# Six output weights split by GpSimd and an adding transfer, and spare splits bound in order behind block splits, in a two-layer encoder kernel

## The chip, the cores and the metric

The kernel runs on one core of one Trainium2 chip. The metric is the device time of one execution in microseconds (us). Several executions of a kernel are timed; one further execution was recorded by the hardware profiler, and all views of the profile come from that one. The engines are named as in the profile: PE is TensorE (matmul), PEld its weight loads, DVE is VectorE, ACT is ScalarE, POOL is GpSimd, SP is SyncE, which here only issues transfers (DMAs).

## What is computed

Two layers of an encoder on 512 tokens of width 1024, all in fp32. Layer 0 mixes tokens by banded attention (mixer A), layer 1 by global attention (mixer B); both add attention over 256 memory rows, an output product with `w_o`, and a SwiGLU feed-forward part.

```python
for i in range(DEPTH):                                   # DEPTH = 2
    h = rms_norm(x, g_mix_pre[i])
    proj = h @ w_in[i]                                   # q, k, v, memory q
    tok = mixer_a(...) if i == 0 else mixer_b(...)       # 12 heads of 64, 3 kv heads
    mo = memory_attention(qm, km, vm)                    # 4 heads
    o = jnp.concatenate([tok, mo], axis=-1) @ w_o[i]
    x = x + rms_norm(o, g_mix_post[i])
    h = rms_norm(x, g_ffn_pre[i])
    gu = h @ w_gate_up[i]
    f = (jax.nn.silu(gu[..., :D_FF]) * gu[..., D_FF:]) @ w_down[i]   # D_FF = 2816
    x = x + rms_norm(f, g_ffn_post[i])
```

## The kernel before

**Splits.** Every fp32 operand of a large product is split into a high part, which is the operand rounded to the matmul's narrower format (`fp32r`), and a low part, which is what is left. A product is then three matmuls: high by high, high by low, low by high (`mm3`, L308 to L310; L1131 to L1133 and L1257 to L1259 in the feed-forward part). The helper `split` (L313) makes the parts: ACT copies the source into the high tile (L318), and DVE subtracts the high tile from the source (L322). A flag moves the first to POOL (L316) or the second (L320). The weights' parts are tiles `whi` and `wlo` with four buffers each, taken in turn, so a new pair waits until PE has done with the pair four before. The unsplit weight comes from HBM by a transfer that SP issues, into a tile `raw`.

**Order.** PE's instructions run in the order in which the program writes them. All other engines take their instructions in an order that a scheduler made ahead of time, and each engine works through its list strictly in order: an instruction that waits holds up all behind it. An edge `issue_after(a)` tells the scheduler to place an instruction behind `a`.

**Mixers.** In each layer the heads' pieces (scores, softmax, transposes, values) are laid on one axis `x`, one unit for a head, by `put(x, f)` and written out in that order. `PACE` holds the places for each layer. The first half of the output product (`heads_out`, L837) is laid among the last heads: four weight units `wo[0..3]` of 128 x 1024 are loaded and split by `unit` at `ow` = 10.3, 10.8, 12.2, 13.2 (layer 0), the second half of each split a quarter unit later, and `owm` picks the engines (0: ACT and DVE). The products with units 0 to 2 start at `ox` = 11.4; unit 3 is used in `mix_out`, after the heads. In layer 1, units 0 and 1 come ready split from HBM (below); only units 2 and 3 are split there. POOL's work in this stage is the softmax's division (L663, tile `p`), four instructions a head.

**Feed-forward.** The 22 columns of 128 hidden values are worked through in four lots (`LOTS`). Lots 1 and 2 use a seven-product scheme (`seven`, L1125, for the first product). Such a lot ends with `down(h)` (L1314), the second product by the same scheme: seven stages of `times` (L1252) named A11, A12, S2, S1, S3, S4, A22, each of 18 matmuls on `fp32r` parts of a weight block. The blocks `b11`, `b21`, `t2`, `t1`, `t3`, `b22`, `t4` come from HBM into tiles `rb`, `ru`, `raw` (1024 wide) and `rs` (512 wide), some as sums made by an adding transfer that POOL issues (L1082); `pairs` (L1243) splits each. The hidden values of the lot's last column are still made by ACT (SiLU, L1184; high part, L1007) and DVE while A12 begins; the last third of A12 needs them.

**Spare pairs, in layer 0 only.** While layer 0 runs, weights of layer 1 are loaded, split and stored as pairs in HBM, for layer 1 to fetch. In each of lots 1 and 2, `spare_load` (L1295) loads two units of `in_wq` into `raw` during A12, and `spare_pair` (L1302), twice, splits one unit in two halves through tiles `c` (high) and `s` (low), two buffers each, and stores the four halves (`pair<-c`, `pair<-s`). The split is the same helper, so its rows have lines L318 and L322 with tile names `c` and `s`. In `down` the two calls of `spare_pair` stand behind the products S1 and S4 (L1333 and L1340). After the lot's A22 the next lot begins with `p1` and `p2` (L1139, L1144), which need the pair `a`, split from `raw`.

Of the kernel before, what the change touches and what calls it, by code (L numbers as in the profile page):

```python
# [28 lines left out]
NF = DFF // P  # L29
EPS = 1e-6  # L30
NPART = 2
WPART = 2
BIG = 1e37
NFILL = 3
# [9 lines left out]
LOTS = ((0, 2), (2, 8), (8, 14), (14, 22))  # L44
SEVEN, HALF = (1, 2), 3

PACE = [{'lag': 1.692, 'vlag': 0.479, 'jstep': 0.213, 'kstep': 0.375, 'klag': 0.742, 'qoff': [0.212, 0.126, 0.099], 'qlag': 1.02, 'late': 0.6, 'moff': -0.235, 'mdur': 0.562, 'mlag': 0.697, 'kw': [0, 0, 0, 0], 'mw': [2, 1, 1, 0], 'qw': [0, 0, 0, 1, 3, 3, 3, 3], 'hoff': 0, 'ow': [10.3, 10.8, 12.2, 13.2], 'ox': 11.4, 'od': 0.3, 'hstep': 0.872, 'hlag': 1.742, 'hjstep': 0.135, 'hvlag': 0.751, 'owm': [0, 0, 0, 0, 0, 0, 0, 0], 'q0step': 0.27, 'q0off': -0.032, 'q0lag': 0.919, 'm0off': -0.078, 'm0dur': 0.002, 'm0lead': 1.887, 'mlead': 1.201, 'qlead': 0.921, 'q0lead': 1.555, 'qstep': 1.002, 'tw': [0, 0, 0, 0, 0, 0, 0, 0], 'h2off': 0}, {'lag': 1.824, 'vlag': 0.535, 'jstep': 0.218, 'kstep': 0.777, 'klag': 1.715, 'qoff': [-0.027, -0.162, -0.027], 'qlag': 1.189, 'late': 2.15, 'moff': -0.088, 'mdur': 0.384, 'mlag': 1.205, 'kw': [0, 0, 0, 0], 'mw': [0, 0, 0, 0], 'qw': [0, 0, 0, 0, 0, 3, 1, 1], 'hoff': 0, 'ow': [10.2, 10.7, 12.2, 13.2], 'ox': 11.3, 'od': 0.3, 'hstep': 0.946, 'hlag': 1.847, 'hjstep': 0.295, 'hvlag': 0.568, 'owm': [0, 0, 0, 0, 0, 0, 0, 0], 'q0step': 0.718, 'q0off': -0.018, 'q0lag': 1.136, 'm0off': -1.059, 'm0dur': 0.171, 'm0lead': 2.465, 'mlead': 3.162, 'qlead': 1.895, 'q0lead': 1.42, 'qstep': 0.998, 'tw': [0, 0, 0, 0, 0, 0, 0, 0], 'h2off': 0.016}]

# [155 lines left out]
class Trunk:  # L204
# [39 lines left out]
    def unit(self, src, side=0, pool=None, parts=1, put=None, x=0, dst=None, key=None, g=None, raw=None, pair=None, early=None):  # L244


        nc, n = self.nc, src.shape[-1]
        own = raw or self.early.pop(early, None)
        if pair in self.pairs:
            def fetch():  # L250
                dst[key] = [self.whl.tile([P, 1024], F32R, tag=z, name=f"w{z}", bufs=4) for z in ("hi", "lo")]
                for z in range(2):
                    nc.sync.dma_start(dst[key][z].bitcast(F32), self.pairs[pair][z])

            put(x, fetch)
# [612 lines left out]
    def mix_out(self, l, forms, resid, dst):  # L868
# [115 lines left out]
    def ffn(self, l, pools, forms, late, done):  # L984
# [235 lines left out]
        for k in range(2):  # L1220
            c = slice(512 * k, 512 * k + 512)
# [21 lines left out]
        def pairs(t):  # L1243
            out = []
            for x in t:
                n = x.shape[-1]
                hi, lo = [self.whl.tile([P, 1024], F32R, tag=z, name=f"w{z}", bufs=4) for z in ("hi", "lo")]
                self.split(hi[:, :n], lo[:, :n], x)
                out.append((hi, lo))
            return out  # L1250

        def times(ps, h, name, pr, steps, fresh):  # L1252
            mm = nc.tensor.matmul
            for i, t in steps:
                lh, ll = block(h["lot"], name, 0, i, t), block(h["lot"], name, 1, i, t)
                rh, rl = [pr[i // 2][z][:, i % 2 * 512:i % 2 * 512 + 512] for z in range(2)]
                mm(ps[t], lh, rh, start=fresh and i == 0, stop=False, skip_group_check=True)  # L1257
                mm(ps[t], lh, rl, start=False, stop=False, skip_group_check=True)  # L1258
                mm(ps[t], ll, rh, start=False, stop=i == HALF - 1, skip_group_check=True)  # L1259
# [42 lines left out]
        def spare_pair():  # L1302
            if spares:
                x, name, *at = spares.pop(0)
                self.pairs[(name, *at)] = y = [self.dram.tile([P, 1024], F32, name="pair", tag="_".join(map(str, (name, z, *at))))
                                               for z in range(2)]
                for z in range(2):
                    c = slice(512 * z, 512 * z + 512)
                    hi, lo = temp("c"), temp("s")
                    self.split(hi.bitcast(F32R), lo.bitcast(F32R), x[:, c])  # L1310
                    queue(nc.sync, y[0][:, c], hi)
                    queue(nc.sync, y[1][:, c], lo)

        def down(h):  # L1314

            x = h["x"]
            due()
            out_of(x, 0, 0)
            w = pairs(h["b21"])
            z = [self.tagged("s"), self.tagged("s")]  # L1320
            times(z, h, "A12", w, BY_UNIT, True)
            spare_load()
            spare_load()
            down_load(h, 3)
            rope()
            out_of(z, 0, 0)
            w = pairs(h["t2"])
            times(x, h, "S2", w, BY_UNIT, False)
            out_of(x, 0, 1, True)
            w = pairs(h["t1"])  # L1330
            y = [self.tagged("pv"), self.tagged("t")]
            times(y, h, "S1", w, BY_ROW, True)
            spare_pair()  # L1333
            out_of(y, 1, 1)
            w = pairs(h["t3"])
            times(x, h, "S3", w, BY_ROW, False)
            out_of(x, 1, 1, True)
            w = pairs(h["b22"])
            times(y, h, "S4", w, BY_ROW, False)
            spare_pair()  # L1340
            out_of(y, 0, 1)
            w = pairs(h["t4"])
            times(x, h, "A22", w, BY_ROW, False)
            out_of(x, 1, 0)

        for c, (f0, f1) in list(enumerate(LOTS))[1:]:
# [40 lines left out]
            if c in SEVEN:  # L1387
                down(head)
# [221 lines left out]
```

## Time and profile before

| | |
|---|---|
| median of 3 runs | 1089.26 us (1089.0 to 1090.06) |
| the profiled execution, as timed | 1091.68 us |
| its span in the profile | 1089.9 us |
| granted TensorE clock, mean over the span | 0.994 |
| busy: ACT, POOL | 693.5 us, 255.3 us |

A profile row of the timeline gives start, duration, engine, line, operation, output and inputs; in brackets stand the engine's idle time just before and what ended it. The table by windows gives each engine's busy time in a stretch, the number of instructions in brackets, then the clock granted to PE (1.00 is full), the busy share of the 16 DMA engines and GB/s. PE is busy nearly throughout, so a change of time is a change of PE's waits or of its clock.

### The profile page before, as it was taken

What the parts mean: (1) busy time and instruction counts of PE and PEld (TensorE: products, weight loads), DVE (VectorE), ACT (ScalarE), POOL (GpSimd) and SP (SyncE); (2) the same over time, 40 slices, a digit from 0 to 9 for tenths busy, and PEclk for the clock granted to TensorE, in tenths of its full rate; (3) what the DMA queues carried; (4) which work ended last, traced back from release to release, by engine and by line L of the source; (5) the groups of instructions that cost most, each with busy time, mean ns of one, the idle gap of its engine ahead of it and who ended that gap; (6) DMA issues with size and microseconds to landing.
All of it is one profiled execution on the core that took longest, in us unless ns stands there. A gap on an engine that the chain in (4) does not pass through costs nothing.

```text
span 1089.9 us, 19990 instructions
## 1 busy us (share of the span) xinstructions
PE 1063.6 (98%) x7364; PEld 973.2 (89%) x7364; DVE 894.2 (82%) x1561; ACT 693.5 (64%) x1429; POOL 255.3 (23%) x405
## 2 busy tenths in 40 slices
PE   9999999999999989999999999999999999999997
PEld 7899887999879979998898888778999899899986
DVE  7889875978899979995887998767979888899954
ACT  7679884766646645663566888766766466556631
POOL 5673331211131100000443553313011111100001
PEclk9999999999999999999999999999999999999999
DMA  9721106456987894329752220136369769833243
GB/s 326 265 67 39 33 20 258 148 134 173 264 272 181 233 273 166 110 67 317 242 193 98 78 78 1 47 119 227 104 149 261 219 162 255 220 113 105 68 162 116
DMA packets 56978, 173.42 MB, mean 159 GB/s; under 512 B 6576, under 2 KB 6960, under 8 KB 56752
## 3 DMA queue, kind: packets, MB, share of 16 engines
q1 hardware_dynamic: 47376, 150.76, 40.4%
q0 software_dynamic: 9216, 20.98, 11.4%
q8 instruction: 58, 0.95, 0.4%
q10 hardware_dynamic: 288, 0.40, 0.1%
q14 instruction: 40, 0.33, 0.1%
HBM read 149.04 MB, written 16.78 MB: 152 GB/s over the span
## 4 chain that ended last, share of the span: by engine, by line
PE 82%; DVE 7%; ACT 4%; DMA 3%; issue 2%; POOL 2%; SPq 0%; DVEq 0%; POOLq 0%; ACTq 0%
PE ps L1131 11%; PE ps L1132 11%; PE ps L1133 11%; PE ps L309 9%; PE ps L308 9%; PE ps L310 9%; PE ps L1259 3%; PE ps L1257 3%; PE ps L1258 3%; PE tp L673 3%; PE o L687 2%; PE o L688 2%; PE s L612 1%; DMA raw<-in_wq_dram 1%; PE s L613 1%
## 5 line engine op out<-in xcount | busy, mean ns | idle before, releaser
L318 ACT ACTIVATE whi<-raw 128x512 fp32r<-128x512 f32 (+3 forms) x180 | 141.2, 804 | 93.6 <-issue 26.0
L322 DVE TENSOR_TENSOR wlo<-raw,whi 128x512 fp32r<-128x512 f32 (+3 forms) x176 | 157.8, 912 | 38.3 <-ACT whi L318 37.8
L1131 PE MATMUL ps<-hrows,whi 128*128 128x256 f32 x640 | 176.3, 275 | 0.1
L1132 PE MATMUL ps<-hrows,wlo 128*128 128x256 f32 x640 | 176.2, 275 | 0.0
L1133 PE MATMUL ps<-hrows,whi 128*128 128x256 f32 x640 | 176.2, 275 | 0.0
L308 PE MATMUL ps<-whi,hrows 128*128 128x256 f32 (+2 forms) x432 | 144.1, 333 | 0.0
L309 PE MATMUL ps<-wlo,hrows 128*128 128x256 f32 (+2 forms) x432 | 138.0, 319 | 1.6 <-DVE wlo L322 1.5
L310 PE MATMUL ps<-whi,hrows 128*128 128x256 f32 (+2 forms) x432 | 138.0, 320 | 0.0
L1132 PE MATMUL ps<-a,wlo 128*128 128x256 f32 x480 | 132.1, 275 | 0.0
L1131 PE MATMUL ps<-a,whi 128*128 128x256 f32 x480 | 132.1, 275 | 0.0
L1133 PE MATMUL ps<-a,whi 128*128 128x256 f32 x480 | 132.1, 275 | 0.0
L1131 PEld LDWEIGHTS ps<-hrows,whi 128*128 128x128 f32 x640 | 120.1, 188 | 0.8 <-ACT p L1137 0.3
L1132 PEld LDWEIGHTS ps<-hrows,wlo 128*128 128x128 f32 x640 | 120.1, 188 | 0.5
L1133 PEld LDWEIGHTS ps<-hrows,whi 128*128 128x128 f32 x640 | 120.1, 188 | 0.0
L663 POOL TENSOR_SCALAR p<-p,rd 128x256 f32<-128x256 f32 (+2 forms) x128 | 78.1, 628 | 102.8 <-DVE rd L660 66.2
L1132 PEld LDWEIGHTS ps<-a,wlo 128*128 128x128 f32 x480 | 90.1, 188 | 0.2
L1131 PEld LDWEIGHTS ps<-a,whi 128*128 128x128 f32 x480 | 90.1, 188 | 0.2
L1133 PEld LDWEIGHTS ps<-a,whi 128*128 128x128 f32 x480 | 90.1, 188 | 0.0
L309 PEld LDWEIGHTS ps<-wlo,hrows 128*128 128x128 f32 x432 | 81.6, 189 | 7.4 <-DVE wlo L322 2.5
L310 PEld LDWEIGHTS ps<-whi,hrows 128*128 128x128 f32 x432 | 81.3, 188 | 5.6 <-DVE hrows L336 0.3
L308 PEld LDWEIGHTS ps<-whi,hrows 128*128 128x128 f32 x432 | 81.4, 188 | 5.0
L318 ACT ACTIVATE whi<-rb 128x1024 fp32r<-128x1024 f32 x56 | 59.6, 1064 | 29.9 <-PE ps L1259 20.7
(231 smaller groups left out, 2854.0 us busy)
## 6 DMA issues: line engine op xcount, KB each, us to landing
raw<-in_wgu_dram SPq DMA_DIRECT2D x48, 512.0 KB, 4.6
rb<-in_wgu_dram SPq DMA_DIRECT2D x40, 512.0 KB, 3.9
raw<-in_wd_dram SPq DMA_DIRECT2D x18, 512.0 KB, 4.3
raw<-in_wq_dram SPq DMA_DIRECT2D x16, 512.0 KB, 5.3
raw<-in_wo_dram SPq DMA_DIRECT2D x16, 512.0 KB, 3.6
rb<-in_ws_dram SPq DMA_DIRECT2D x16, 512.0 KB, 7.6
rs<-in_ws_dram SPq DMA_DIRECT2D x28, 256.0 KB, 6.5
xt<-x SPq DMA_DIRECT2D x12, 512.0 KB, 4.9
```

The costliest lines, as they stand in the source:

```text
L308: mm(out, lh, rh, start=first, stop=False)
L309: mm(out, lh, rl, start=False, stop=False)
L310: mm(out, ll, rh, start=False, stop=last)
L318: a = nc.scalar.activation(hi, src, AF.Copy)
L322: b = nc.vector.tensor_sub(lo, src, hi.bitcast(F32))
L663: self.pooled = nc.gpsimd.tensor_scalar(hd["p"][z][:, :n], hd["p"][z][:, :n], rd[:, z:z + 1], 1.0, op0=OP.mult, op1=OP.mult)
L673: nc.tensor.transpose(tp[:, z], hd["p"][i][:, jj * P:(jj + 1) * P], self.ident)
L1131: mm(out, wh[:, s], rh, start=start and k == 0, stop=False, skip_group_check=True)
L1132: mm(out, wl[:, s], rh, start=False, stop=False, skip_group_check=True)
L1133: mm(out, wh[:, s], rl, start=False, stop=k == 3, skip_group_check=True)
L1257: mm(ps[t], lh, rh, start=fresh and i == 0, stop=False, skip_group_check=True)
L1258: mm(ps[t], lh, rl, start=False, stop=False, skip_group_check=True)
```

## The change

**Output weights.** Units with `owm` = 4 take another way through `unit`: all four in layer 0, units 2 and 3 in layer 1, so six. At `x - 0.8` (`EARLY`) the tiles are taken and SP issues the load. Then, for each half, ACT copies the high part as before, and POOL writes the negative of the high part into the low tile. After the second half POOL issues an adding transfer that adds the raw weight (512 KB, from on-chip memory to on-chip memory) to the low tile. DVE has no part in it.

**Spare pairs.** In `down` the two calls of `spare_pair` move one place: behind `pairs(h["t3"])` and behind `pairs(h["t4"])`, so behind the lot's next block split instead of ahead of it. `pairs` and `spare_pair` keep the last split's two instructions in `ends["pair"]`, and each spare split is bound behind both by order edges.

```diff
+EARLY = 0.8
 PACE, layer 0:
-'owm': [0, 0, 0, 0, 0, 0, 0, 0]
+'owm': [4, 4, 4, 4, 0, 0, 0, 0]
 PACE, layer 1:
-'owm': [0, 0, 0, 0, 0, 0, 0, 0]
+'owm': [0, 0, 4, 4, 0, 0, 0, 0]
...
+        def turned_over():
+            hi, lo = dst[key] = [self.whl.tile([P, 1024], F32R, tag=z, name=f"w{z}", bufs=4) for z in ("hi", "lo")]
+            own = self.raw()
+            nc.sync.dma_start(own[:, :n], src)
+            box.append((hi, lo, own))
+
+        def high(z):
+            hi, lo, own = box[0]
+            c = slice(z * n // NPART, (z + 1) * n // NPART)
+            nc.scalar.activation(hi[:, c], own[:, c], AF.Copy)
+            nc.gpsimd.tensor_scalar(lo[:, c], hi[:, c].bitcast(F32), -1.0, 1.0, op0=OP.mult, op1=OP.mult)
+            if z == NPART - 1:
+                nc.gpsimd.dma_start(lo[:, :n], own[:, :n].bitcast(F32R), accum_op=OP.add, max_dma_last_dim=4096)
+
+        if side == 4:
+            put(x - EARLY, turned_over)
+            for z in range(NPART):
+                put(x - EARLY + 0.01 + z / 4, lambda z=z: high(z))
+            return
...
-                self.split(hi[:, :n], lo[:, :n], x)
+                ends["pair"] = self.split(hi[:, :n], lo[:, :n], x)
...
-                    self.split(hi.bitcast(F32R), lo.bitcast(F32R), x[:, c])
+                    a, b = ends["pair"]
+                    with self.tc.issue_after(a), self.tc.issue_after(b):
+                        ends["pair"] = self.split(hi.bitcast(F32R), lo.bitcast(F32R), x[:, c])
...
             times(y, h, "S1", w, BY_ROW, True)
-            spare_pair()
             out_of(y, 1, 1)
             w = pairs(h["t3"])
+            spare_pair()
             times(x, h, "S3", w, BY_ROW, False)
...
             times(y, h, "S4", w, BY_ROW, False)
-            spare_pair()
             out_of(y, 0, 1)
             w = pairs(h["t4"])
+            spare_pair()
             times(x, h, "A22", w, BY_ROW, False)
```

PE's list is the same row for row; what moves stands on the other engines. Lines behind the new code are 21 higher in the changed kernel up to `pairs` (so L322 becomes L343), and the new code is L297 (ACT), L298 and L300 (POOL).

ACT, in layer 0 at the end of lot 1, from the splits of `b21` on, before. `c<-raw` is a spare split, `whi<-ru` the split of `t2` and then of `t1`, `s<-ps` the SiLU of the lot's last column and `f<-s` the high part of its hidden values:

```order
L318 ACTIVATE whi<-rs 128x512
L318 ACTIVATE c<-raw 128x512
L318 ACTIVATE whi<-ru 128x1024
L1184 ACTIVATE s<-ps 128x256
L318 ACTIVATE whi<-rs 128x512
L1007 ACTIVATE f_4231<-s 128x512
L318 ACTIVATE c<-raw 128x512
L318 ACTIVATE whi<-ru 128x1024
```

The same place in the changed kernel, to the first two spare splits (the rows between are the splits of `t1` and `t3`):

```order
L339 ACTIVATE whi<-rs 128x512
L339 ACTIVATE whi<-ru 128x1024
L1205 ACTIVATE s<-ps 128x256
L339 ACTIVATE whi<-rs 128x512
L1028 ACTIVATE f_4235<-s 128x512
L339 ACTIVATE whi<-ru 128x1024
L339 ACTIVATE f_4242<-q 128x512
L1028 ACTIVATE f_4247<-k 128x256
L339 ACTIVATE whi<-rs 128x512
L339 ACTIVATE whi<-rb 128x1024
L339 ACTIVATE whi<-rs 128x512
L339 ACTIVATE c<-raw 128x512 x2
```

The two spare splits of the first call have moved from ahead of the SiLU and of `t1` to behind the split of `t3`. The second call's two stand in the changed kernel behind the splits of `t4`, just ahead of the next lot's `whi<-raw`. Lot 2 reads alike.

DVE, in layer 0's mixer among the last heads, where the output product begins, before. `tl<-tp,th` is the low part of a turned softmax tile, `p,nm` the masked scores, `tok` a head's result:

```order
L322 TENSOR_TENSOR hrows<-tok,hrows 128x512
L322 TENSOR_TENSOR wlo<-raw,whi 128x512
L322 TENSOR_TENSOR tl<-tp,th 128x256
L618 ISA p,nm<-s,mask,nsink 128x256
L618 ISA nm 128x1
L696 TENSOR_TENSOR tok<-o,tmp 64x512
L618 ISA p,nm<-s,mask,nsink 128x256
L618 ISA nm 128x1
L659 TENSOR_TENSOR den<-den,es 128x4
L322 TENSOR_TENSOR wlo<-raw,whi 128x512
L660 RECIPROCAL rd<-den 128x4
L322 TENSOR_TENSOR tl<-tp,th 128x384 x2
```

The same place in the changed kernel:

```order
L639 ISA p,nm<-s,mask,nsink 128x256
L639 ISA nm 128x1
L343 TENSOR_TENSOR tl<-tp,th 128x256
L717 TENSOR_TENSOR tok<-o,tmp 64x512
L639 ISA p,nm<-s,mask,nsink 128x256
L639 ISA nm 128x1
L680 TENSOR_TENSOR den<-den,es 128x4
L681 RECIPROCAL rd<-den 128x4
L343 TENSOR_TENSOR tl<-tp,th 128x384
```

The two weight splits are gone from DVE, and the split of a finished head (`hrows<-tok`) has moved further back, on ACT too.

POOL, in layer 0's mixer around the third and fourth output weight of the changed kernel (before, the rows L663 followed one another without any between):

```order
L684 TENSOR_SCALAR p<-p,rd 128x256
L298 TENSOR_SCALAR wlo<-whi 128x512 x2
L300 DMA wlo<-raw 128x1024
L684 TENSOR_SCALAR p<-p,rd 128x256
L684 TENSOR_SCALAR p<-p,rd 128x384 x2
L684 TENSOR_SCALAR p<-p,rd 128x256
L298 TENSOR_SCALAR wlo<-whi 128x512 x2
L684 TENSOR_SCALAR p<-p,rd 128x256
L684 TENSOR_SCALAR p<-p,rd 128x384 x2
L684 TENSOR_SCALAR p<-p,rd 128x256
L300 DMA wlo<-raw 128x1024
```

The new instructions stand between one head's four divisions and the next head's, and the fourth weight's transfer a head later than its negatives.

More of the change, by code (lines that the diff above doesn't have):

```diff
@@ L45 @@
 SEVEN, HALF = (1, 2), 3
-PACE = [{'lag': 1.692, 'vlag': 0.479, 'jstep': 0.213, 'kstep': 0.375, 'klag': 0.742, 'qoff': [0.212, 0.126, 0.099], 'qlag': 1.02, 'late': 0.6, 'moff': -0.235, 'mdur': 0.562, 'mlag': 0.697, 'kw': [0, 0, 0, 0], 'mw': [2, 1, 1, 0], 'qw': [0, 0, 0, 1, 3, 3, 3, 3], 'hoff': 0, 'ow': [10.3, 10.8, 12.2, 13.2], 'ox': 11.4, 'od': 0.3, 'hstep': 0.872, 'hlag': 1.742, 'hjstep': 0.135, 'hvlag': 0.751, 'owm': [0, 0, 0, 0, 0, 0, 0, 0], 'q0step': 0.27, 'q0off': -0.032, 'q0lag': 0.919, 'm0off': -0.078, 'm0dur': 0.002, 'm0lead': 1.887, 'mlead': 1.201, 'qlead': 0.921, 'q0lead': 1.555, 'qstep': 1.002, 'tw': [0, 0, 0, 0, 0, 0, 0, 0], 'h2off': 0}, {'lag': 1.824, 'vlag': 0.535, 'jstep': 0.218, 'kstep': 0.777, 'klag': 1.715, 'qoff': [-0.027, -0.162, -0.027], 'qlag': 1.189, 'late': 2.15, 'moff': -0.088, 'mdur': 0.384, 'mlag': 1.205, 'kw': [0, 0, 0, 0], 'mw': [0, 0, 0, 0], 'qw': [0, 0, 0, 0, 0, 3, 1, 1], 'hoff': 0, 'ow': [10.2, 10.7, 12.2, 13.2], 'ox': 11.3, 'od': 0.3, 'hstep': 0.946, 'hlag': 1.847, 'hjstep': 0.295, 'hvlag': 0.568, 'owm': [0, 0, 0, 0, 0, 0, 0, 0], 'q0step': 0.718, 'q0off': -0.018, 'q0lag': 1.136, 'm0off': -1.059, 'm0dur': 0.171, 'm0lead': 2.465, 'mlead': 3.162, 'qlead': 1.895, 'q0lead': 1.42, 'qstep': 0.998, 'tw': [0, 0, 0, 0, 0, 0, 0, 0], 'h2off': 0.016}]
@@ new lines @@
+PACE = [{'lag': 1.692, 'vlag': 0.479, 'jstep': 0.213, 'kstep': 0.375, 'klag': 0.742, 'qoff': [0.212, 0.126, 0.099], 'qlag': 1.02, 'late': 0.6, 'moff': -0.235, 'mdur': 0.562, 'mlag': 0.697, 'kw': [0, 0, 0, 0], 'mw': [2, 1, 1, 0], 'qw': [0, 0, 0, 1, 3, 3, 3, 3], 'hoff': 0, 'ow': [10.3, 10.8, 12.2, 13.2], 'ox': 11.4, 'od': 0.3, 'hstep': 0.872, 'hlag': 1.742, 'hjstep': 0.135, 'hvlag': 0.751, 'owm': [4, 4, 4, 4, 0, 0, 0, 0], 'q0step': 0.27, 'q0off': -0.032, 'q0lag': 0.919, 'm0off': -0.078, 'm0dur': 0.002, 'm0lead': 1.887, 'mlead': 1.201, 'qlead': 0.921, 'q0lead': 1.555, 'qstep': 1.002, 'tw': [0, 0, 0, 0, 0, 0, 0, 0], 'h2off': 0}, {'lag': 1.824, 'vlag': 0.535, 'jstep': 0.218, 'kstep': 0.777, 'klag': 1.715, 'qoff': [-0.027, -0.162, -0.027], 'qlag': 1.189, 'late': 2.15, 'moff': -0.088, 'mdur': 0.384, 'mlag': 1.205, 'kw': [0, 0, 0, 0], 'mw': [0, 0, 0, 0], 'qw': [0, 0, 0, 0, 0, 3, 1, 1], 'hoff': 0, 'ow': [10.2, 10.7, 12.2, 13.2], 'ox': 11.3, 'od': 0.3, 'hstep': 0.946, 'hlag': 1.847, 'hjstep': 0.295, 'hvlag': 0.568, 'owm': [0, 0, 4, 4, 0, 0, 0, 0], 'q0step': 0.718, 'q0off': -0.018, 'q0lag': 1.136, 'm0off': -1.059, 'm0dur': 0.171, 'm0lead': 2.465, 'mlead': 3.162, 'qlead': 1.895, 'q0lead': 1.42, 'qstep': 0.998, 'tw': [0, 0, 0, 0, 0, 0, 0, 0], 'h2off': 0.016}]
```

## The prediction

> **What bounds the kernel now.** I read the page first, then PE's waits, then what ended them.
>
> ```profile
> span 1089.9 us, 19990 instructions
> PE 1063.6 (98%) x7364; PEld 973.2 (89%) x7364; DVE 894.2 (82%) x1561; ACT 693.5 (64%) x1429; POOL 255.3 (23%) x405
> ```
>
> PE is busy for 98% of the span, so only the 26 us between 1089.9 and 1063.6, and stretches of low clock, can be won. DVE is next with 82%. The list of PE's waits says where the idle time is, and ACT's list has one odd row:
>
> ```profile
> PE ps L1257 <- ACT f L1007: 5.5, 2, 2.9
> PE tp L673 <- DVE tl L322: 3.8, 8, 1.4
> ...
> ACT c L318 <- DMA raw<-in_wq_dram: 6.9, 2, 3.6
> ACT c L318 <- DMA pair<-c: 5.4, 3, 3.0
> ```
>
> The costliest wait comes only twice: the second-product matmuls (L1257) wait for hidden values. ACT waits twice, too, for a spare weight. ACT's timeline at the end of layer 0's lot 1 joins the two:
>
> ```profile
> 297.33 0.63 ACT L318 ACTIVATE c<-raw 128x512 fp32r<-128x512 f32 x1 [3.59 <-DMA raw<-in_wq_dram]
> 297.87 1.04 ACT L318 ACTIVATE whi<-ru 128x1024 fp32r<-128x1024 f32 x1
> 298.82 0.36 ACT L1184 ACTIVATE s<-ps 128x256 f32<-128x256 f32 x1
> ...
> 300.80 0.63 ACT L1007 ACTIVATE f<-s 128x512 fp32r<-128x512 f32 x1 [1.11 <-DVE s L1185]
> ```
>
> ACT takes its list in order. A spare split waited 3.59 us for its load, and the SiLU behind it (298.82) came late, though PE had left its product for A12 at 295.67 (below). PE then stood. These are the first matmul of A12, the one after the gap and the first of the next lot, for lot 1, for lot 2, and for lot 1 of layer 1, which has the same stages but no spare pairs:
>
> ```profile
> 295.67 0.39 PE L1257 MATMUL ps<-whi,f 128*128 128x512 f32 x1
> 301.49 0.50 PE L1257 MATMUL ps<-whi,f 128*128 128x512 f32 x1 [2.91 <-ACT f L1007]
> 325.42 0.28 PE L1131 MATMUL ps<-a,whi 128*128 128x256 f32 x1
> 387.33 0.39 PE L1257 MATMUL ps<-whi,f 128*128 128x512 f32 x1
> 392.87 0.50 PE L1257 MATMUL ps<-whi,f 128*128 128x512 f32 x1 [2.63 <-ACT f L1007]
> 416.82 0.28 PE L1131 MATMUL ps<-a,whi 128*128 128x256 f32 x1
> 851.62 0.39 PE L1257 MATMUL ps<-whi,f 128*128 128x512 f32 x1
> 876.46 0.28 PE L1131 MATMUL ps<-a,whi 128*128 128x256 f32 x1
> ```
>
> The same 108 matmuls take 29.75 us (295.67 to 325.42), 29.49 us (387.33 to 416.82) and, undisturbed, 24.84 us (851.62 to 876.46). Layer 0 loses 4.91 + 4.65 = **9.56 us** here, more than the idle time of 2.91 + 2.63 = 5.54. The windows after the gaps hold the rest:
>
> ```profile
> 302.00:304.00 2.00, 1.85 (x5) 1.35 (x5) 1.81 (x5) 1.73 (x3) 0.19 (x1) 0.61 1.13 258
> 304.00:306.00 2.00, 2.00 (x6) 1.54 (x6) 2.00 (x4) 0.63 (x1) 0.69 (x1) 0.54 1.04 202
> ...
> 394.00:396.00 2.00, 2.00 (x7) 1.58 (x7) 2.00 (x6) 1.74 (x4) 0.88 (x1) 0.65 1.06 223
> 396.00:398.00 2.00, 2.00 (x6) 1.51 (x6) 2.00 (x3) 0.00 (x0) 0.00 (x0) 0.50 0.91 165
> ```
>
> PE's granted clock falls to 0.61, 0.54, 0.65 and 0.50. That is (0.39 + 0.46) x 2 = 1.7 us lost in lot 1 and (0.35 + 0.50) x 2 = 1.7 in lot 2.
>
> The Trainium skill, page "TensorE: Matmul & The Clock Gate", section "What's actually happening", has the clock halved only after an idle window of about 3.4 us. The trace does not agree: idle gaps of 2.91 and 2.63 us were enough. By the rule the dips would not hang on these gaps, and only 5.5 of the 9.56 us would come back. That result is a rival below.
>
> **The change, part by part.**
>
> *Spare pairs.* With the spare split behind `t3`, the SiLU can start when its product is done, about 2.9 us earlier than 298.82. The high part then comes at about 297.9, and A12 needs it 12 matmuls after 295.67, at 298.4. The wait is gone, as in layer 1, and with it the dips. What is late next is DVE and the transfers:
>
> ```profile
> 284.50:325.42 40.92, 37.86 (x188) 31.55 (x187) 34.07 (x53) 18.82 (x30) 11.46 (x13) 0.96 0.90 262
> 843.20:876.46 33.26, 33.26 (x164) 27.71 (x163) 30.39 (x48) 15.96 (x23) 4.99 (x6) 1.00 0.78 209
> ...
> L322 DVE TENSOR_TENSOR s<-raw,c 128x512 fp32r<-128x512 f32 x8 | 5.8, 723 | 6.2 <-ACT c L318 6.2
> ```
>
> In layer 1's undisturbed stretch DVE has 33.26 - 30.39 = 2.87 us to spare, and layer 0 has four spare splits of 0.72 us more: 2.9 us. Nothing is left. Likewise the DMA engines: 0.90 x 40.92 = 36.8 us of work, which then has 40.92 - 4.91 = 36.0 us. The cost lies between 0 (what doesn't fit slides into the next lot's columns) and 2.9 us a lot. I take 0.6 a lot, nearer to 0, because the order puts two of the next lot's sums behind its first weight split. Gain 9.56 - 1.2 = **8.4 us**.
>
> The second call's copies now stand just ahead of the next lot's `whi<-raw` on ACT. They need the two `c` buffers back from the first call's stores, for which ACT waited at most 3.0 us before. Two stages, 36 of the 108 matmuls or 8.3 us, lie between the calls, so I cost it at nothing; if that cover goes, the first rival has the price. On SP, loads of the next lot now stand between the first call's stores; they need tiles that the splits of `t3` and `b22` release, which are no later than before.
>
> *Output weights, layer 0.* Twelve DVE splits go (eight here, four in layer 1); POOL gets twelve one-input instructions and six issues, DMA six on-chip transfers. The nearest rows:
>
> ```profile
> L322 DVE TENSOR_TENSOR wlo<-raw,whi 128x512 fp32r<-128x512 f32 x94 | 62.3, 687 | 0.6 <-ACT whi L318 0.2
> L316 POOL TENSOR_SCALAR whi<-raw 128x512 fp32r<-128x512 f32 x10 | 6.1, 628 | 0.0
> L320 POOL TENSOR_TENSOR wlo<-raw,whi 128x512 fp32r<-128x512 f32 x14 | 18.5, 1335 | 2.9 <-ACT whi L318 2.9
> L1079 POOL DMA_DIRECT2D ru<-ru x4 | 3.5, 872 | 29.2 <-DMA ru<-in_ws_dram 13.9 <-DVE wlo L322 7.7 <-DVE c L1178 7.6
> ...
> ru<-ru POOLq DMA_DIRECT2D x4, 512.0 KB, 5.1
> ```
>
> DVE loses 12 x 0.687 = 8.2 us of work; POOL gains 2 x 0.628 + 0.872 = 2.13 us a weight. The low part is whole 5.1 us after the issue.
>
> The Trainium skill, "GPSIMD Engine Reference", section "Engine selection", speaks against elementwise work on POOL: about twice DVE's time with two inputs, near DVE's with one. The trace agrees: 1335 ns against 687, but 628 for one input. At the two-input price twelve would cost POOL 16.0 us, not 7.5; the change uses the other form.
>
> What DVE's relief is worth is read where PE waits for it:
>
> ```profile
> 130.33 0.69 DVE L322 TENSOR_TENSOR wlo<-raw,whi 128x512 fp32r<-128x512 f32 x1
> 131.02 1.04 DVE L322 TENSOR_TENSOR tl<-tp,th 128x384 fp32r<-128x384 f32 x2
> ...
> 131.70 0.40 PE L673 MATMUL tp<-cst,p 128*128 128x128 f32 x1 [1.37 <-DVE tl L322]
> ...
> 123.09 2.05 POOL L663 TENSOR_SCALAR p<-p,rd 128x256 f32<-128x256 f32 x4 [4.67 <-PE tp L673]
> ...
> 132.00:134.00 2.00, 2.00 (x7) 1.75 (x6) 1.50 (x5) 1.91 (x6) 1.52 (x3) 0.50 0.84 254
> 134.00:136.00 2.00, 2.00 (x10) 1.84 (x9) 0.98 (x3) 0.68 (x2) 0.00 (x0) 0.71 0.02 8
> ...
> 692.00:694.00 2.00, 1.44 (x10) 1.21 (x11) 1.75 (x4) 1.72 (x6) 0.30 (x1) 1.00 0.02 6
> ```
>
> A weight split stands right ahead of the low part for which PE waits 1.37 us, and the clock then falls to 0.50 and 0.71: 1.0 + 0.58 = 1.6 us. Without the split (about 0.6 us in place), and with one head split fewer ahead on ACT (a 128x512 copy, 0.63 as at 297.33, some 0.4 of it on this path), the wait shrinks by 1.0 to about 0.4. In the window from 692 PE is idle for 0.56 us and the clock stays at 1.00, so I let the dip go: 1.0 + 1.6 = **2.6 us**. Bounds: -1 (POOL, the last rival, in part) to 3.0.
>
> *Output weights, layer 1.*
>
> ```profile
> 687.78 1.28 DVE L322 TENSOR_TENSOR wlo<-raw,whi 128x512 fp32r<-128x512 f32 x2
> 692.56 0.33 PE L673 MATMUL tp<-cst,p 128*128 128x128 f32 x1 [0.64 <-DVE tl L322]
> ```
>
> Two of the four splits stand 5 us ahead of a 0.64 us wait for DVE. I take it and a little more: **0.8 us**; bounds -1 and 1.3.
>
> *The low parts' lateness* I cost at nothing. In the order the third weight's transfer stands right behind the divisions of 123.09 us; its first use comes 12 products into the output product, which begins behind the transpose of 131.70. Landing takes 5.1.
>
> The sum is 8.4 + 2.6 + 0.8 = 11.8 us. Against the profiled execution that is 1091.68 - 11.8 = 1079.9. The median of the runs lies 2.4 lower (0.2%), so I forecast 1089.3 - 11.8 = **1077.5 us**.
>
> **The rivals.**
>
> *A new wait at the next lot's head (chance 0.14).* DVE or the stores of the first spare pair are late, `whi<-raw` and its low part miss PE's first need, and PE idles again. For it: DVE and DMA have nothing to spare (2.87 against 2.9; 36.8 against 36.0). Against it: what is late can slide by 20 us of columns. Price up to 2.9 + 1.7 a lot, 9.2 in all; half of it beyond my 1.2 is the middle: 1077.5 + 4 = 1081.5, up to 1085.5.
>
> *The mixers give nothing (0.08)*, the change does not do there what it says, because ACT and not DVE is the bound: ACT is busy for 1.91 of the 2.00 us from 132. Time 1077.5 + 3.4 = 1080.9.
>
> *The clock still falls (0.04)*: the gaps go, the dips stay, since something else sets them. Then 3.4 + 1.6 us stay: 1082.5.
>
> *POOL's list holds up the heads (0.06): slower.* Each new group stands ahead of a head's divisions, on which the transposes wait. The shortest gap into which it must fit:
>
> ```profile
> 109.64 2.23 POOL L663 TENSOR_SCALAR p<-p,rd 128x256 f32<-128x256 f32 x4 [3.75 <-DVE rd L660]
> ```
>
> The group's 2.13 us fits into 3.75, with 1.6 to spare. If ACT's high part or the load comes more than 1.6 us into the gap, the divisions wait. At the full 2.13 us for six weights that is 12.8 us, against the lots' 8.4: 1089.3 - 8.4 + 12.8 = 1093.7.
>
> **How the numbers follow.** The forecast has 0.68; the rivals share 0.32. The range reaches from 1074.5 (nothing lost in the lots, upper bounds in the mixers: 9.56 + 3.0 + 1.3 = 13.9, and 0.9 for the runs' spread) to 1083.5, which takes in the second and third rival and most of the first. A measurement here tells about 0.2%, 2.2 us, from no change. Faster by more: the forecast and nearly all of the first three rivals, 0.91; within: 0.04, from the first rival's end and a weak form of the last; slower: 0.05.
>
> **What would show it.** In the profile after, the 108 matmuls of lots 1 and 2 should take 24.8 to 26 us with the clock at 1.00, and no ACT wait for `raw<-in_wq`. Near 130 us PE's wait for `tl` should be under 0.7 us and no window at 0.5. The divisions on POOL should still wait for DVE's `rd`. I am wrong if PE idles at the first `ps<-a,whi` after A22, or if `tp` waits for POOL.

## The result, and the profile after

| | before | changed |
|---|---|---|
| first comparison, median | 1089.26 us (7 runs) | 1084.82 us (7 runs) |
| ratio, with its 95% interval | | 0.9964 (0.9949 to 0.9979) |
| second comparison, median | 1088.29 us (29 runs) | 1086.9 us (12 runs) |
| ratio, with its 95% interval | | 0.9987 (0.9977 to 0.9997) |
| first profiled execution, as timed | 1091.68 us | 1085.38 us |

The changed kernel is faster by 0.1% (1.4 us) in one comparison and by 0.4% (4.4 us) in the other, whose intervals barely meet, and not by the 11.8 us of the forecast; the time lies above the range's end of 1083.5. Span and busy times of its profile, to be laid beside those of before:

```profile
span 1083.6 us, 19994 instructions
PE 1059.2 (98%) x7364; PEld 969.5 (89%) x7364; DVE 888.6 (82%) x1549; ACT 693.9 (64%) x1429; POOL 263.5 (24%) x423
```

DVE lost its twelve splits (1561 to 1549 instructions, and 5.6 us of busy time) and POOL got eighteen instructions, as the change says. PE is as full as it was. PE's list of waits (total in us, times, longest):

```profile
PE ps L1279 <- DVE wlo L343: 3.3, 2, 2.5
PE tp L694 <- DVE tl L343: 2.0, 6, 0.7
PE o L708 <- DVE tok L717: 1.9, 4, 0.7
PE ps L1152 <- ACT p L1158: 1.3, 2, 0.7
PE ps L330 <- DVE wlo L343: 1.3, 2, 0.8
PE ps L539 <- ACT whi L339: 1.2, 1, 1.2
PE ps L329 <- ACT whi L339: 1.2, 1, 1.2
```

The wait of the second product for `f`, 5.5 us before, is gone, and the waits for `tl` fell from 3.8 to 2.0. Three are new beside the first profile of before: the second product waits for a low part (L1279, 3.3 us), the next lot for a copy `p` (L1152, 1.3), and at the end of layer 0 a projection waits for its weight (L329, 1.2). PE's timeline, first matmul of A12, the new gap, first of the next lot, for lots 1 and 2:

```profile
293.46 0.39 PE L1278 MATMUL ps<-whi,f 128*128 128x512 f32 x1
317.08 0.50 PE L1279 MATMUL ps<-wlo,f 128*128 128x512 f32 x1 [2.52 <-DVE wlo L343]
321.07 0.28 PE L1152 MATMUL ps<-a,whi 128*128 128x256 f32 x1
383.74 0.39 PE L1278 MATMUL ps<-whi,f 128*128 128x512 f32 x1
405.60 0.50 PE L1279 MATMUL ps<-wlo,f 128*128 128x512 f32 x1 [0.77 <-DVE wlo L343]
409.59 0.28 PE L1152 MATMUL ps<-a,whi 128*128 128x256 f32 x1
```

The 108 matmuls take 27.61 us (293.46 to 321.07) and 25.85 us, not 24.8. The stages up to S4 run without a wait; the gap is inside A22, which waits for the low part of `t4`. The timelines of DVE and of SP's transfers say why that part is late in lot 1:

```profile
313.88 0.69 DVE L1130 TENSOR_TENSOR ru<-raw,rb 128x512 f32<-128x512 f32 x1 [3.27 <-DMA rb<-in_wgu_dram]
314.61 0.69 DVE L1131 TENSOR_TENSOR rb<-rb 128x512 f32<-128x512 f32 x1
315.21 0.68 DVE L1288 TENSOR_TENSOR o<-o,ps 128x512 f32<-128x512 f32 x1
315.81 1.22 DVE L343 TENSOR_TENSOR wlo<-rb,whi 128x1024 fp32r<-128x1024 f32 x1
...
307.29 0.38 SPq L1100 DMA_DIRECT2D pair<-c  x1
307.78 0.36 SPq L1122 DMA_DIRECT2D rb<-in_wgu_dram  x1
```

In DVE's list the two sums for the next lot's first column (L1130, L1131) stand ahead of the low part of `t4` (315.81). They need a load `rb`, which SP issued at 307.78 and which DVE had 6.1 us later. DVE stood 3.27 us for it, with the split that PE needs ready behind. The same place in the timelines of before:

```profile
318.36 0.81 DVE L1109 TENSOR_TENSOR ru<-raw,rb 128x512 f32<-128x512 f32 x1
319.08 0.68 DVE L1267 TENSOR_TENSOR o<-o,ps 128x512 f32<-128x512 f32 x1
319.68 1.21 DVE L322 TENSOR_TENSOR wlo<-rb,whi 128x1024 fp32r<-128x1024 f32 x1
...
321.57 0.39 PE L1258 MATMUL ps<-wlo,f 128*128 128x512 f32 x1
...
314.03 0.37 SPq L1101 DMA_DIRECT2D rb<-in_wgu_dram  x1
```

A sum stood there too, but the load had landed after 4.3 us, and the low part was ready at 320.89, 0.7 us ahead of its first matmul at 321.57. In the changed kernel PE came to that matmul at 314.56 (317.08 less 2.52), 7.0 us earlier; the load was issued 6.3 us earlier, took 1.8 us longer, and one more sum stands in front.

The traces can be laid side by side, since PE's matmuls stand in one order in all kernels: this table gives the time between the same two matmuls in each, in us; the stages are named by their times in the first profile of before, and only those that differ are listed. "Again" is a second profiled execution of an unaltered kernel (e6, e5 below).

| stage | before | before again | changed | changed again | pairs only (e1) | weights only (e2) |
|---|---|---|---|---|---|---|
| start to 100 | 98.83 | 97.88 | 98.16 | 97.72 | 97.97 | 97.70 |
| mixer 0, 100 to 185 | 85.18 | 83.76 | 83.43 | 83.42 | 83.75 | 83.35 |
| lot 1 up to S4, 280 to 320 | 40.13 | 37.94 | 35.16 | 35.18 | 35.17 | 38.17 |
| A22 and next columns, 320 to 340 | 19.80 | 20.40 | 23.38 | 24.50 | 22.23 | 20.70 |
| lot 2, A11 to S2, 380 to 400 | 19.85 | 19.26 | 15.16 | 15.17 | 15.17 | 19.16 |
| rest of lot 2 and next columns, 400 to 420 | 19.99 | 19.99 | 22.15 | 21.56 | 21.71 | 19.99 |
| end of layer 0, 500 to 560 | 60.07 | 60.37 | 60.80 | 63.39 | 63.17 | 60.70 |
| mixer 1, 640 to 720 | 80.04 | 80.09 | 79.17 | 79.15 | 80.08 | 79.17 |

All other stages of these six profiles agree within 0.3 us. Against the first profile of before, the lots gain 4.97 + 4.69 = 9.66 us up to the last stages and give back 3.58 + 2.16 = 5.74 behind them; the mixers gain 1.75 + 0.87; the end of layer 0 loses 0.73.

### The profile page after: what moved, and what is told of

The parts are those of the page before. It is cut to its first block, busy times and chain, and to the rows that moved or that the text cites. A ratio compares the mean times of both kernels' runs of the same rounds, so it can differ in the third digit from the quotient of the medians.

```text
span 1083.6 us, 19994 instructions
## 1 busy us (share of the span) xinstructions
PE 1059.2 (98%) x7364; PEld 969.5 (89%) x7364; DVE 888.6 (82%) x1549; ACT 693.9 (64%) x1429; POOL 263.5 (24%) x423
## 4 chain that ended last, share of the span: by engine, by line
PE 80%; DVE 8%; ACT 4%; DMA 3%; issue 2%; POOL 2%; DVEq 0%; SPq 0%; ACTq 0%; POOLq 0%
PE ps L1154 12%; PE ps L1152 12%; PE ps L1153 12%; PE ps L330 9%; PE ps L329 9%; PE ps L331 9%; PE tp L694 3%; PE ps L1280 3%; PE ps L1279 3%; PE ps L1278 2%; PE o L708 2%; PE o L709 2%; DVE wlo L343 2%; PE s L633 1%; PE s L634 1%
## 5 line engine op out<-in xcount | busy, mean ns | idle before, releaser
L339 ACT ACTIVATE whi<-raw 128x512 fp32r<-128x512 f32 (+3 forms) x168 | 133.5, 815 | 91.9 <-issue 26.8
L343 DVE TENSOR_TENSOR wlo<-raw,whi 128x512 fp32r<-128x512 f32 (+3 forms) x164 | 149.9, 930 | 39.3 <-ACT whi L339 38.8
L1152 PE MATMUL ps<-hrows,whi 128*128 128x256 f32 x640 | 176.4, 276 | 1.3 <-ACT p L1158 1.3
L329 PE MATMUL ps<-whi,hrows 128*128 128x256 f32 (+2 forms) x432 | 143.9, 333 | 1.2 <-ACT whi L339 1.2
L1152 PE MATMUL ps<-a,whi 128*128 128x256 f32 x480 | 132.1, 275 | 0.0
L1152 PEld LDWEIGHTS ps<-hrows,whi 128*128 128x128 f32 x640 | 120.1, 188 | 2.2 <-ACT p L1158 1.7
L1152 PEld LDWEIGHTS ps<-a,whi 128*128 128x128 f32 x480 | 90.1, 188 | 0.2
L329 PEld LDWEIGHTS ps<-whi,hrows 128*128 128x128 f32 x432 | 81.3, 188 | 6.4 <-ACT whi L339 1.5
```

The costliest lines, as they stand in the source:

```text
L329: mm(out, lh, rh, start=first, stop=False)
L339: a = nc.scalar.activation(hi, src, AF.Copy)
L343: b = nc.vector.tensor_sub(lo, src, hi.bitcast(F32))
L1152: mm(out, wh[:, s], rh, start=start and k == 0, stop=False, skip_group_check=True)
```

## The experiments

**The kernels unaltered, once more (e6, e5).**

> The kernel before, unaltered: a second profile of it, and what this comparison shows of no change. If the low clock in layer 0's two lots and mixer belongs to the waits (as the prediction had it), the 108 matmuls take 29.5 us in both lots again; if the first profile was a slow execution (it was 1091.68, 2.4 above its median), one or both take some 27 to 28, as lot 2 did in the run with the weights alone. The ratio: 1.000 within 0.15%.

Measured: 1088.18 us, ratio 1.0002 (0.9994 to 1.0011). Its profile has its waits in the same places as the first, but those for `f` are shorter (1.72 and 2.18 us against 2.91 and 2.63), and the clock is not the same. Its timeline of PE, from A12 to the next lot in lot 1, and the mixer's wait:

```profile
293.28 0.39 PE L1257 MATMUL ps<-whi,f 128*128 128x512 f32 x1
297.91 0.50 PE L1257 MATMUL ps<-whi,f 128*128 128x512 f32 x1 [1.72 <-ACT f L1007]
320.95 0.28 PE L1131 MATMUL ps<-a,whi 128*128 128x256 f32 x1
...
130.78 0.41 PE L673 MATMUL tp<-cst,p 128*128 128x128 f32 x2 [1.35 <-DVE tl L322]
```

And its windows behind the waits of the mixer, of lot 1 and of lot 2 (the third column from the right is PE's clock):

```profile
132.00:134.00 2.00, 2.00 (x14) 1.79 (x13) 1.85 (x6) 1.85 (x6) 0.60 (x1) 1.00 0.49 197
...
298.00:300.00 2.00, 1.86 (x7) 1.25 (x8) 2.00 (x6) 2.00 (x4) 0.00 (x0) 1.00 1.10 268
...
388.00:390.00 2.00, 1.42 (x4) 0.88 (x5) 1.94 (x5) 2.00 (x4) 0.30 (x1) 0.76 1.13 249
390.00:392.00 2.00, 2.00 (x6) 1.57 (x5) 1.85 (x4) 1.25 (x3) 0.88 (x1) 0.50 1.02 211
```

In lot 1 the clock stays at 1.00 and the 108 matmuls take 27.67 us; in lot 2 it falls to 0.76 and 0.50 (28.89 us). In the mixer the wait is 1.35 us, as before, and the clock does not fall. The first profile of before had three dips, this one has one. A dip costs about 1.7 us, and two of them are most of the 4.2 us by which the first execution was the longer (1091.68 against 1087.48); the shorter waits for `f` are another 1.6.

> The changed kernel unaltered, for a second profiled execution and a time beside the other variants. If the waits are the kernel's own: A22 waits 2.5 us for wlo in lot 1 and 0.8 in lot 2 again, and the fourth wkv load at the end of layer 0 lands 4.9 us after its issue (as it did in all four profiles with the spare pairs at their new places: 4.9, 5.0, 5.6, 4.9), with a ratio to before near 0.9965. If the late landing is chance: 3.3 us, as before, and a time some 1 to 3 us lower.

Measured: the second comparison above. The waits come again, though not in the same sizes: A22 waits 3.2 and 0.2 us for `wlo` (2.5 and 0.8 in the first profile), and the `wkv` load at the end of layer 0 lands 5.4 us after its issue. The clock fell twice, behind the gap in A22 of lot 1 and at the end of layer 0, as two of its windows show:

```profile
318.00:320.00 2.00, 2.00 (x6) 1.55 (x5) 2.00 (x4) 0.00 (x0) 0.00 (x0) 0.50 0.10 39
...
540.00:542.00 2.00, 2.00 (x8) 2.00 (x8) 1.52 (x4) 0.66 (x2) 0.47 (x1) 0.50 0.76 199
```

No dip came in the first profile of the changed kernel. Of the 6.3 us between the first two profiled executions (1091.68 and 1085.38), some 5 are therefore dips: three against none.

**The two parts (e1, e2).** The edits: for e1 all `owm` back to 0; for e2 the two calls of `spare_pair` at their old places and the split without edges.

> Only the spare pairs' new places and edges; the output weights are split as before. Theory 1 (the lots gain what the prediction took off, and give part of it back because VectorE's list holds t4's low part behind an addition that waits for the next lot's rb load): the pieces A12 to S4 are some 4.7 us a lot shorter than before, and some 3.6 and 2.2 us come back between A22 and the next lot's second column; net about -3.9 us, near 1085.4. Theory 2 (the give-back was chance of one profiled execution): net -8 us or more, near 1081. The waits of layer 0's mixer stay as in the kernel before.

Measured: 1088.45 us, ratio 1.0008 (0.9999 to 1.0016). The pairs alone gain nothing; both theories forecast less. Against the second profile of before, the stages show how: they gain 2.77 + 4.09 = 6.86 us in the lots, and give back 1.83 and 1.72 behind them and 2.80 at the end of layer 0, 6.35 together. Neither theory had the last.

> Only the low parts of the six output weights on the new path; the spare pairs stand where they stood, without edges. By the stages of the two profiles: -1.7 us in layer 0's mixer and -0.9 in layer 1's, near 1086.7; the two lots keep 29.5 us for the 108 matmuls. If the new path gives nothing, 1089; if it gives what the prediction said (3.4), 1085.9.

Measured: 1087.22 us, ratio 0.9993 (0.9985 to 1.0002). Layer 1's mixer is 0.92 us shorter than in the second profile of before and layer 0's 0.41; the lots keep their gaps. The expected 1.7 for layer 0 was mostly a clock dip of the first profile. Multiplied, the two parts give 1.0001, and the whole 0.9964 and 0.9987: that the whole gains more than its parts is not explained. Executions of the changed kernel lay between 1083.92 and 1089.8 us in the second comparison.

**VectorE's list behind t4 (e3, repeated as e12).** The sums for the next lot's first column are bound behind the split of `t4`:

```diff
-                ends["pair"] = self.split(hi[:, :n], lo[:, :n], x)
+                ends["pair"] = ends["unit"] = self.split(hi[:, :n], lo[:, :n], x)
...
-        def load_b(f):
+        def load_b(f, unit=None):
...
+                    self.tc.issue_after(unit[1]) if unit else nullcontext():
...
-            load_b(gs[0])
+            load_b(gs[0], ends.get("unit"))
```

> The changed kernel, with the two additions on the next lot's rb bound behind the split of t4, so that VectorE splits t4 before it waits for the load. Theory 1: no wait for wlo in A22; of the 3.6 and 2.2 us given back about 0.9 a lot stays (the copy of p behind the later addition of ru): some 4 us below the changed kernel, near 1081. Rival (VectorE or the DMA engines have no room, so that the wait only moves to the next lot's first columns): within 1 us of the changed kernel, 1084 to 1085.5.

> The additions behind the split of t4 unaltered, beside the two above: 0.996 of before in its first comparison; a profile with a landing of 4.9 to 5.6 us. If the comparisons differ among themselves by more than their intervals, it shows here too.

Measured: 1083.87 us, 0.996 (0.9948 to 0.9973), and 1082.45 us, 0.9948 (0.9931 to 0.9964). PE's timeline, first matmul of A12 and of the next lot, lots 1 and 2, and the one wait behind lot 1:

```profile
293.07 0.39 PE L1279 MATMUL ps<-whi,f 128*128 128x512 f32 x1
317.86 0.28 PE L1153 MATMUL ps<-a,whi 128*128 128x256 f32 x1
381.41 0.39 PE L1279 MATMUL ps<-whi,f 128*128 128x512 f32 x1
406.21 0.28 PE L1153 MATMUL ps<-a,whi 128*128 128x256 f32 x1
...
322.51 0.38 PE L1153 MATMUL ps<-hrows,whi 128*128 128x256 f32 x1 [1.73 <-ACT p L1159]
```

The 108 matmuls take 24.79 and 24.80 us, the undisturbed 24.84 of layer 1. So neither DVE nor the DMA engines lacked room for them; the order alone made the wait. Behind lot 1 the later sums hold up a copy (1.73 us), behind lot 2 no wait is left. Against the second profile of before, the stages behind the lots lose 1.05 and 0.22 us in e3 and 0.53 and 0.21 in e12. The times say less than the profiles: the forecast was some 4 us below the changed kernel, and 1083.87 us alone is near the rival's 1084; 1082.45 lies below it.

What is left behind lot 1 goes with the second spare pair. ACT's second copy of that call stood for a buffer `c`, which the first call's stores give back:

```profile
314.31 0.63 ACT L339 ACTIVATE c<-raw 128x512 fp32r<-128x512 f32 x1 [2.48 <-DMA pair<-c]
```

DVE's low part of it, the sums and the copy come behind. Behind lot 1, ACT's wait was 2.48 us in e3 and 2.73 in e12, and the copy made PE wait 1.73 and 1.21; behind lot 2 ACT waited 1.29 and 1.25, and PE not at all. No run changes this wait by itself.

**The load by another queue (e4).** The first `rb` load of the next lot is taken out of `prep_a` and issued by `nc.gpsimd.dma_start` behind the split of `t3`.

> The changed kernel, with the next lot's first rb load issued by GpSimd's queue right behind t3's split instead of by SP behind the first spare pair's first store; VectorE's list is as in the changed kernel. Theory 1 with the load's lateness as its root: the issue moves from 307.8 to about 304.5 us (lot 1), the landing from 313.9 to about 310.5, the wait of VectorE's addition falls from 3.3 to under 1 us, and A22's wait for wlo goes; 3 to 4 us below the changed kernel, near 1081.5. Rival (DMA engines full, the load only takes the place of another that is then late): within 1 us of the changed kernel.

Measured: 1091.81 us, 1.0035 (1.0017 to 1.0053). The edit missed its aim: the scheduler put the issue behind other work of POOL. Rows of POOL, DVE and PE in lot 1:

```profile
312.21 0.61 POOL L1116 DMA_DIRECT2D rb<-in_wgu_dram  x1
...
318.14 0.69 DVE L1134 TENSOR_TENSOR ru<-raw,rb 128x512 f32<-128x512 f32 x1 [8.86 <-DMA rb<-in_wgu_dram]
...
321.34 0.80 PE L1283 MATMUL ps<-wlo,f 128*128 128x512 f32 x1 [7.47 <-DVE wlo L343]
```

The later load is a measure of the same cause. DVE's wait for `rb` and PE's gap in A22, in four places: 0.36 and 0 us (lot 2 of e9), 2.58 and 0.77 (lot 2, changed), 3.27 and 2.52 (lot 1, changed), 8.86 and 7.47 (here). PE pays for what DVE waits beyond some 0.8 to 1.8 us. Why the load of lot 2 lands 4.4 us after its issue in e9 and 6.4 and 5.8 in the two profiles of the changed kernel is not known.

**Other orders (e7, e8).** e7 keeps the edges and puts the calls of `spare_pair` back to their old places. e8 is e3 with the second call moved on:

```diff
             w = pairs(h["t4"])
-            spare_pair()
...
             prep_c(gs[0])
+            if c > 1:
+                ends["pair"] = ends["col"]
+                spare_pair()
```

> The changed kernel with the spare pairs' calls at the places of before, but with the edges: each pair stands right behind the split of t1 and of b22 in ScalarE's and VectorE's lists, and t4's low part stands ahead of the additions that wait for rb. Theory 1 (the order decides, not the room): no wait of 2.5 us for f, none for wlo in A22; up to 1.3 us a lot is lost at S3, whose t3 now stands behind the first pair; time from 1082.5 to 1085.5, at or below the changed kernel. Rival (the places make the gain): the wait for f returns, 1087.

> The changed kernel with the two additions behind the split of t4, and the second spare pair behind the next lot's second weight split, so that its wait for the stores of the first pair holds up neither the next lot's first weights nor its additions. Theory 1: the 1.65 us that came back in lot 1 in the run with the additions alone shrinks to under 0.8; 1082.5 to 1083.5. Rival: the copy of p behind the second pair's copies is late, 0.5 to 1 us a lot worse than the additions alone, 1084.5 to 1085.5.

Measured: e7 1088.68 us, 1.0005 (0.9994 to 1.0016); e8 1092.23 us, 1.0037 (1.0024 to 1.005). Both expectations were wrong. DVE and PE behind lot 1, first e7, then e8:

```profile
317.84 0.69 DVE L1130 TENSOR_TENSOR ru<-raw,rb 128x512 f32<-128x512 f32 x1 [2.07 <-DMA rb<-in_wgu_dram]
...
320.32 0.38 PE L1153 MATMUL ps<-a,wlo 128*128 128x256 f32 x1 [2.04 <-DVE wlo L343]
```

```profile
317.74 0.69 DVE L1131 TENSOR_TENSOR ru<-raw,rb 128x512 f32<-128x512 f32 x1 [3.91 <-DMA rb<-in_wgu_dram]
...
320.22 0.39 PE L1154 MATMUL ps<-a,wlo 128*128 128x256 f32 x1 [2.20 <-DVE wlo L343]
```

It is the same mechanism one place on. The scheduler put the sum of the lot's second column ahead of the low part of the first column's weights, and DVE stood for that column's `rb`. So an edge at one place moved the wait to the next.

**The end of layer 0 (e9, e10, e11).** In all eight profiles with the spare pairs' edges and 12 warming matmuls, the fourth `wkv` load lands 4.9 to 5.6 us after its issue; in the three without (before twice, e2) after 3.3 to 3.5. SP issues it at the same place of PE's list. Issue and the split that waits for the load, in the timelines of the changed kernel and of before:

```profile
531.33 0.33 SPq L263 DMA_DIRECT2D raw<-in_wkv_dram  x1
536.21 0.84 ACT L339 ACTIVATE whi<-raw 128x768 fp32r<-128x768 f32 x1 [2.73 <-DMA raw<-in_wkv_dram]
```

```profile
537.91 0.33 SPq L262 DMA_DIRECT2D raw<-in_wkv_dram  x1
541.24 0.85 ACT L318 ACTIVATE whi<-raw 128x768 fp32r<-128x768 f32 x1 [1.18 <-DMA raw<-in_wkv_dram]
```

The view of the DMA queues (packets, MB, share of 16 engines) tells what else moves. First the changed kernel from 533.0 to 533.5 us, then before from 541.1 to 541.5:

```profile
q8 instruction: 1, 0.02, 12.1%
```

```profile
q8 instruction: 1, 0.02, 15.2%
```

Queue q8 moves 58 packets of 16 KB in a run, and PE's stream has 7364 weight loads, 7364 matmuls and about 100 semaphore instructions: one packet for every 256. In the changed kernel one such packet starts 1.7 to 2.2 us after the load's issue, while the load's packets are under way (by its record it runs from 1.99 to 2.96 us after); in before 3.2 to 3.6 us after, when they are through. Of the load's 128 packets in the changed kernel, 122 start within 2 us; the last six start 2.15 to 2.83 us after the first, one behind the other, so I take them for part of one DMA engine's share (the records name no engine). That engine's packets begin again as the q8 packet ends: in the changed kernel 2.95 us after the issue, and in all eight late profiles and in e11 (below) within 0.02 us of that end. In before all start within 1.41. The trace holds 47 semaphore instructions in PE's stream ahead of this place in before, 49 with the weights alone, 51 with the pairs alone and 53 with both. The row listing of PE is the same; the stream is not.

The Trainium skill, page "Advanced Engine Details and Errata", section "ISA Cache", gives cache lines of 16 KB, 256 instructions each; the count of packets agrees. Its page "DMA: Bandwidth & Descriptors", section "Queues, rings and completion order", has each DMA engine take its queues in turn, a packet at a time; that fits one engine's share of the load held up by one packet.

To move the packet without touching the load, the number of warming matmuls at the start was changed (two instructions each): `busy(12)` to `busy(10)` in the changed kernel (e9) and in e3 (e10), to `busy(14)` in before (e11).

> The changed kernel with 10 instead of 12 warming matmuls at the very start: TensorE's instruction stream is 4 instructions shorter from there on, which takes back the 4 semaphore instructions that the moved spare pairs add to it. Theory 3 (the late landing at the end of layer 0 is a 16 KB packet of instructions, which TensorE's stream draws every 256 instructions, and which now comes on one DMA engine 1.5 us after the fourth wkv load is issued instead of 3.3 us, ahead of that engine's share of the load): the packet comes 3 us or more after the issue again, the load lands in 3.3 us, and 1.4 to 3.2 us go, most of them in the stage at 525 to 560 us: near 0.9965 to 0.998 of before. Rival (the landing hangs on the order of loads and stores in the lots): 4.9 us as in five profiles of the moved pairs, 0.9987 as in the second comparison.

> The same with the two additions behind the split of t4: by theory 1 and theory 3 together the stage at the end of layer 0 loses 3 us against the run with the additions alone, 1081 to 1082 us, some 0.6% below before. If only theory 1 holds, as the additions alone, 1083.9.

> The kernel before with 14 instead of 12 warming matmuls: 4 instructions more in TensorE's stream. Theory 3: the fourth wkv load lands 4.9 us or later after its issue, TensorE waits 1.2 to 1.7 us at the end of layer 0, and the time is 1.3 to 3 us above before, 1.0012 to 1.0028. Rival: landing 3.3 us, 1.000.

Rows of ACT in e9 and in e11; the loads were issued at 529.08 and 536.89:

```profile
532.59 0.85 ACT L339 ACTIVATE whi<-raw 128x768 fp32r<-128x768 f32 x1 [1.37 <-DMA raw<-in_wkv_dram]
```

```profile
541.91 0.84 ACT L318 ACTIVATE whi<-raw 128x768 fp32r<-128x768 f32 x1 [2.88 <-DMA raw<-in_wkv_dram]
```

Landing follows the stream: 3.5 us in e9 and 3.2 in e10 with four instructions less, 5.0 in e11 with four more. The stage from 500 to 560 us takes 60.09 in e9 and 60.28 in e10, against 60.80 to 63.39 in the changed kernel and 61.49 to 63.90 in e3; in e11 it takes 63.62 against 60.07 and 60.37. Times: e9 1084.81 us, 0.9967 (0.9953 to 0.998); e10 1082.63, 0.9947 (0.9931 to 0.9962); e11 1090.73, 1.002 (1.0006 to 1.0033). The cause of the late landing is shown both ways, and e11 shows its price in time. The time of e9 shows it less well, since the rest of lot 2 was short there too (19.98 us against 22.15 and 21.56). In e10 the stage's gain does not show in the median beside e12 (1082.45). Its profile shows two losses that e12's does not have. PE idles for 2.08 us at 6.9 us, and the clock falls there (0.82 and 0.50 from 6 to 10 us); e9, with the same two matmuls less, idles for 0.96 without a dip. And behind lot 2 the wait of e3's lot 1 comes again, so that the rest of that lot takes 21.99 us, against 20.20 in e12:

```profile
403.27 0.63 ACT L339 ACTIVATE c<-raw 128x512 fp32r<-128x512 f32 x1 [2.60 <-DMA pair<-c]
...
411.21 0.38 PE L1153 MATMUL ps<-hrows,whi 128*128 128x256 f32 x1 [1.72 <-ACT p L1159]
```

The fastest versions are e12 and e10, 0.52 and 0.53% below before.

## Why the prediction was wrong

**The wait for `f`: right in mechanism, too large.** "The wait is gone, as in layer 1, and with it the dips" held: both lots run without a wait up to S4, and ACT no longer waits for a spare weight there. But the 9.56 us came from one execution, in which the waits were long and the clock fell after both of them. In the second profile of before, the same lots hold only 6.88 us to be won (37.94 - 35.16 and 19.26 - 15.16). The sum was then taken off the median although the profiled execution stood 2.4 us above it: that excess was mostly such dips, and they were subtracted once more.

**"I take 0.6 a lot": the failing step.** The lots gave back 3.58 and 2.16 us, and 4.70 and 1.57 in the second profile of the changed kernel. The bounds reached to 2.9 for the wait itself, but the reasoning looked at DVE's room (2.87 against 2.9 us), and e3 shows that room was not the matter. The wait arose because DVE takes its list in order and sums that wait for a load stood ahead of `t4`. The words "which are no later than before", on the loads of the next lot, looked at the wrong thing: the load landed 4.5 us earlier than before (313.88 against 318.36), but PE needed `t4` 7.0 us earlier. This is the first rival (0.14), with its price about right in lot 1 (up to 4.6 a lot), at another place: inside A22, not at the next lot's head. Of the sign that would prove me wrong, PE idle at the first `ps<-a,whi`, the changed kernel showed nothing; in e7 and e8 PE idled near it, at `ps<-a,wlo`.

**The second call's copies, put at nothing.** "Two stages, 36 of the 108 matmuls or 8.3 us, lie between the calls" was no full cover: ACT waited 1.22 us for `pair<-c` in lot 2 of the changed kernel, and 0.5 to 2.9 in other runs with the calls at these places. In e3, e12 and e10 a wait of PE of 1.2 to 1.7 us went with those of 2.5 us and more; in e1 and e9, which have the changed kernel's order, waits as long went with 0.7 at most. No run takes them out alone.

**Layer 0's mixer: 2.6 us, measured 1.75, and 0.3 against the second profile.** The wait for `tl` shrank from 1.37 to 0.68, not to 0.4. The dip of 1.6 us was not always there.

**Layer 1's mixer: 0.8 us, measured 0.87 to 0.94.** Right.

**POOL's list.** The slower rival did not come: PE's wait for POOL's divisions is 0.6 us in all, before and after. The gaps between the divisions had room for the new work.

**The end of layer 0** was in no term and no rival: 0.4 to 3.0 us, by the second profile of before. Nothing in the change touches it; six semaphore instructions more in PE's stream do, four of them from the pairs.

**The sum.** The median missed by 7.3 us (1084.82 against 1077.5). By the first pair of profiles, 4.5 us are what the lots gave back beyond the 1.2, 1.9 come from the first execution of before, which stood 2.4 above its median, while that of the changed kernel stood 0.6 above its own, 0.8 from the mixers and 0.7 from the end of layer 0; the start of the kernel was 0.7 shorter.

## What to carry to other kernels

When a wait is removed, go down each in-order list behind the place and ask of every instruction that waits for a load what stands behind it and how much sooner that is now needed; here room on the engine did not decide it, and an edge that put the needed work first removed the wait (e3). Then look at the next place: in e7 and e8 the wait came back one column on. Take a second profile of the unaltered kernel before adding up gaps: here two of three clock dips were not in it, and the wait in lot 1 was 1.2 us shorter. And count instructions, semaphores too: a few more or less move the fetch of the stream, and a load far from the change can land late.

## What the runs showed of the hardware

A clock dip lasts 3.41 us at half clock in nearly all traces (6.83 us in e4, around the gap of 7.47), as the records of the granted clock show, so it costs 1.7 us where PE is busy. That length agrees with the window of about 3.4 us in the Trainium skill, page "TensorE: Matmul & The Clock Gate", section "What's actually happening". A shorter gap was followed by one in some executions and not in others: the clock fell after 1.37 us (mixer, first profile), 2.18 us (lot 2, second profile) and 1.19 us (end of layer 0, e7), and did not after 1.35 us (mixer, second profile), 2.52 us (lot 1, changed kernel) and 1.18 us (end of layer 0, changed kernel). What decides was not tried.

A 16 KB packet on the queue named instruction held up the last packets of a 384 KB load, and the split that needs the load started 4.9 to 5.6 us after its issue instead of 3.3 to 3.5: 1.4 to 2.3 us later.
